# Layer 0's projection stage as one list schedule, from a transposed x that the host lays out, with the norm factors applied to the results

## The chip, the core and the metric

The kernel runs on one core of a Trainium2 chip. Its engines have queues of their own: PE (TensorE) multiplies, DVE (VectorE), ACT (ScalarE) and POOL (GpSimd) do elementwise work, SP (SyncE) here issues the transfers. The metric is device time in microseconds, the median of a few executions, and each profile is of one execution of the same program. In the names of the profile a weight or activation is called by its tile: `hT` are the normalised activations with the model dimension on partitions, `wr` a weight as loaded, `wh` and `wl` its two parts, `psa` and `psb` the accumulators in PSUM (`psa` two buffers of 1024 columns, `psb` four of 512), `qd`, `kd`, `vd`, `kmem`, `vmem` are scratch tensors in DRAM.

## The reference

A decoder trunk of two layers over 1024 tokens of width 1024, in float32. This case touches what stands ahead of layer 0's attention:

```python
def rms_norm(x, g):
    y = xf * lax.rsqrt(jnp.mean(xf * xf, axis=-1, keepdims=True) + EPS)
    return (y * g.astype(jnp.float32)).astype(x.dtype)

# layer 0
h = rms_norm(x, attn_norm[0])
proj = h @ w_in                     # 12 query heads, 6 kinds of keys/values x 2 groups, 36 gates, 4 memory heads
q, k_slc, k_win = rope(...)         # rotary turn of queries and keys
kc = rope(compress_blocks(k_cmp, cmp_pos[0], cmp_w1[0], ...), cmp_end)
vc = compress_blocks(v_cmp, cmp_pos[1], cmp_w1[1], ...)
gates = jax.nn.sigmoid(gate_logit + gate_b)
# each layer also attends into 256 memory tokens
kv = rms_norm(mem, g_mem) @ w_mem_kv
```

`compress_blocks` takes windows of 32 tokens at a stride of 16, adds a position table, and puts them through a small network of two matrices with a GELU between. The factor of the norm is one number for each token, so it may be applied to a row of h or to the row of a product of h. Attention of layer 0 is then the sum of three branches (compressed, selected, window) with 12 heads; then come the output projection, a gated feed-forward block with a convolution, and layer 1 with attention of another kind.

## The kernel before, in words

Each matrix product is made of three: both operands are split into a rounded upper part (ACT writes it) and the rest (DVE or POOL subtracts), and `mm3` (L245) issues upper x upper, upper x lower and lower x upper at L249, L250 and L251 into one accumulator. So every weight costs an ACT copy and a subtraction before PE can use it.

`layer0_proj` (L1135) does layer 0's projections. The tokens come in eight blocks of 128. For each, `norm_x` squares the rows on ACT with a running sum (L210), makes the factor on DVE and POOL (L211, L213) and multiplies row, factor and gain on DVE (L227); `norm_turn` turns the block by eight PE transposes (L242) and splits it into `hT` (L173, L174). After each block come the products for the values and gates (292 columns, `product`), which go to `vd0` through `store_v`. Then six generators take turns in a fixed string of letters (`order`, in `layer0_proj`): the keys and the first four heads' queries (`rope_proj`, L1019, with the rotary turn at L1033 to L1040 and stores at L1044), the two compress networks (`compress`, L1056, products with 256-column operands called `m`) and the keys and values of the memory for both layers (`mem_kv`, L327). All other order, the loads on SP among it, follows from how the generators are written. Near the end the first unit's keys are fetched (`keys0`, L1255).

Attention of layer 0 is planned: `planned` (L697) turns scores (L413, PE), maxima (L443, DVE), exponentials (ACT), transposes of the probabilities (L533) and value products (L557) into tasks with durations, and `Plan.run` (L82) is a list scheduler that puts them out in the order in which they would start. Each engine has one task at a time, and a task may hold buffers (`psa`, `psb`, `wr`, and so on). Between these tasks stand fillers: the projections of the other eight heads and of the memory queries (`rope_tasks`, L901; `plain_tasks`, L859). The units' loads (queries, keys, values: L1291, L1260, L1298) are tasks of SP, of no duration in the plan, and the first of them waits for a task `start` of 15 us.

Pools of tiles in SBUF hand out buffers; a tile that takes a place over waits for the earlier tile there.

Of the kernel before, what the change touches and what calls it, by code (L numbers as in the profile page):

```python
# [43 lines left out]
class Plan:  # L44
# [18 lines left out]
    def can(self, t):  # L63
        free, held = self.free, self.held
        for a in t["acq"]:
# [4 lines left out]
            elif a == "pb":  # L70
                if held.get("pb") or free["psb"] < 2:
# [10 lines left out]
    def run(self):  # L82
        engines = ("SP", "POOL", "DVE", "ACT", "PE")
# [51 lines left out]
class Trunk:  # L135
    def __init__(self, ctx, tc, a, out):
        self.tc, self.nc, self.a, self.out = tc, tc.nc, a, out
        e = ctx.enter_context
        self.cp = e(tc.tile_pool(name="cp", bufs=1))
        self.wp = e(tc.tile_pool(name="wp", bufs=1))  # L140
        self.hp = e(tc.tile_pool(name="hp", bufs=1))
# [37 lines left out]
    def constants(self):  # L179
# [7 lines left out]
        nc.vector.memset(self.m_cau[:, :S - P], 0.0)  # L187
        self.nhalf = c[:, C_NH:C_NH + 1]

    def masks(self, pool, keep):  # L190
        nc, m = self.nc, pool.tile([P, C_TRI - C_CAU], F32, name="masks")
        nc.sync.dma_start(m, self.a["consts"][:, C_CAU:C_TRI])
        nc.vector.tensor_copy(self.m_cau[:, S - P:], m[:, 0:P])

        self.m_win = keep.tile([P, 5 * P], BF16, name="winb")
        nc.vector.memset(self.m_win[:, P:4 * P], 0.0)
        nc.vector.tensor_copy(self.m_win[:, 0:P], m[:, P:2 * P])
        nc.vector.tensor_copy(self.m_win[:, 4 * P:], m[:, 0:P])
        self.m_cmp = keep.tile([P, NT, 64], BF16, name="cmpb")
        nc.vector.tensor_copy(self.m_cmp, m[:, 2 * P:].rearrange("p (t n) -> p t n", t=NT))  # L200
# [14 lines left out]

    def norm_t(self, pool, x, gb, hi, lo, o):

        self.norm_turn(self.norm_x(pool, x, gb), hi, lo, o)
# [34 lines left out]
    def proj_t(self, wcol, h, chunks=2):  # L253

        a = self.psa()
        for c in range(chunks):
            for kt in range(KT):
                self.mm3(a[:, c * CH:(c + 1) * CH], wcol(kt), (h[c][0][:, kt, :], h[c][1][:, kt, :]), kt == 0, kt == KT - 1)
        return a

# [6 lines left out]

    def load_cols(self, w, c0, width=P):

        raw = self.wraw([P, KT, width])  # L270
        self.nc.sync.dma_start(raw, w[:, c0:c0 + width].rearrange("(k p) n -> p k n", p=P))
        hi, lo = self.whl([P, KT, width])
        self.split(raw, hi, lo)
        return lambda kt: (hi[:, kt, :], lo[:, kt, :])
# [1814 lines left out]
```

## Time and profile before

| | us |
|---|---|
| median of 3 executions (2533.4 to 2538.47) | 2537.28 |
| the profiled execution | 2537.82 |
| its span in the profile | 2536.0 |
| PE busy over the span | 2457.5 (97%) |
| DVE, ACT, POOL busy over the span | 1835.6, 1344.0, 796.4 |
| layer 0's projections, to the last product before the first score | 0 to 181.05 |
| attention of layer 0 with fillers | 183 to 473 |
| attention of layer 0 without fillers | 473 to 620 |

In the views quoted below, a group's row reads: line, engine, operation, output<-inputs, shape, count, then busy time and mean ns of one, then the idle time of the engine just before, with what ended it. A row of the timeline reads: start, duration, engine, line, operation, tiles, shape, count, and in brackets the idle time ahead of it and what released it. A matmul's duration includes its way through the array, so neighbours overlap; starts tell the pace. A wait view has the total, the number of times and the longest. SPq is SP's own queue of issues.

### The profile page before, as it was taken

What the parts mean: (1) busy time and instruction counts of PE and PEld (TensorE: products, weight loads), DVE (VectorE), ACT (ScalarE), POOL (GpSimd) and SP (SyncE); (2) the same over time, 40 slices, a digit from 0 to 9 for tenths busy, and PEclk for the clock granted to TensorE, in tenths of its full rate; (3) what the DMA queues carried; (4) which work ended last, traced back from release to release, by engine and by line L of the source; (5) the groups of instructions that cost most, each with busy time, mean ns of one, the idle gap of its engine ahead of it and who ended that gap; (6) DMA issues with size and microseconds to landing.
All of it is one profiled execution on the core that took longest, in us unless ns stands there. A gap on an engine that the chain in (4) does not pass through costs nothing.

```text
span 2536.0 us, 35681 instructions
## 1 busy us (share of the span) xinstructions
PE 2457.5 (97%) x12306; PEld 2051.9 (81%) x12306; DVE 1835.6 (72%) x3078; ACT 1344.0 (53%) x2565; POOL 796.4 (31%) x722
## 2 busy tenths in 40 slices
PE   7899999988999999999999999999999999999998
PEld 6788888776878888888889988887778888888887
DVE  5648787676377787888765467878477777888766
ACT  5338787686254454454454356767235445445444
POOL 2235555476045554540000000000225455451001
PEclk9999999999999999999999999999999999999999
DMA  8473333344323333358335466665632333338523
GB/s 251 140 218 91 93 108 106 88 138 135 136 83 100 100 112 100 100 174 303 96 125 155 151 184 187 186 195 167 217 111 79 100 109 104 100 108 299 175 92 125
DMA packets 303276, 357.68 MB, mean 141 GB/s; under 512 B 38024, under 2 KB 183288, under 8 KB 303096
## 3 DMA queue, kind: packets, MB, share of 16 engines
q1 hardware_dynamic: 303096, 355.41, 44.4%
q8 instruction: 97, 1.59, 0.3%
q14 instruction: 83, 0.68, 0.1%
HBM read 245.55 MB, written 109.78 MB: 140 GB/s over the span
## 4 chain that ended last, share of the span: by engine, by line
PE 79%; DVE 5%; ACT 4%; DMA 3%; issue 2%; POOL 2%; SPq 1%; POOLq 0%; ACTq 0%; DVEq 0%
PE psa L249 12%; PE psa L250 12%; PE psa L251 12%; PE psb L249 10%; PE psb L251 10%; PE psb L250 9%; PE psa L413 5%; PE psb L533 4%; PE psb L557 4%; DVE pt L547 1%; ACT pt L544 1%; PE psb L1367 1%; DVE ps L443 1%; ACT ps L456 1%; DMA wr<-o 1%
## 5 line engine op out<-in xcount | busy, mean ns | idle before, releaser
L173 ACT ACTIVATE wh<-wr 128x512 fp32r<-128x512 f32 (+2 forms) x240 | 181.9, 761 | 309.7 <-PE psb L251 140.7
L1848 DVE SCALAR_TENSOR_TENSOR v<-u,cw,v 128x1023 f32<-128x1023 f32 (+1 forms) x176 | 274.5, 1559 | 69.0 <-ACT v L1846 68.7
L174 DVE TENSOR_TENSOR wl<-wr,wh 128x512 fp32r<-128x512 f32 (+2 forms) x232 | 224.4, 969 | 115.6 <-ACT wh L173 115.0
L547 DVE TENSOR_TENSOR pt<-psb,pt 128x512 fp32r<-128x512 f32 (+2 forms) x380 | 244.5, 660 | 70.4 <-ACT pt L544 68.6
L1846 ACT ACTIVATE v<-u,cw 128x1024 f32<-128x1024 f32 x88 | 109.6, 1246 | 310.4 <-DVE u L1835 283.8
L544 ACT ACTIVATE pt<-psb 128x512 fp32r<-128x512 f32 (+2 forms) x380 | 212.7, 575 | 108.8 <-PE psb L533 72.9
L557 PE MATMUL psb<-pt,vv 128*128 128x512 f32 (+2 forms) x864 | 244.8, 361 | 11.2 <-DVE pt L547 6.5
L213 POOL TENSOR_TENSOR rs<-ss,consts 128x1 f32<-128x1 f32 x40 | 23.7, 593 | 625.9 <-DVE ss L211 416.0
L249 PE MATMUL psa<-hT,wh 128*128 128x512 f32 x560 | 218.3, 390 | 0.0
L251 PE MATMUL psa<-hT,wl 128*128 128x512 f32 x560 | 218.1, 389 | 0.2 <-DVE wl L174 0.2
L250 PE MATMUL psa<-hT,wh 128*128 128x512 f32 x560 | 217.9, 389 | 0.0
L413 PE MATMUL psa<-kk,qq 128*128 128x512 f32 (+4 forms) x792 | 180.4, 347 | 15.2 <-DVE stat L443 6.1
L557 PEld LDWEIGHTS psb<-pt,vv 128*128 128x128 f32 x864 | 144.8, 190 | 33.0 <-DVE pt L547 12.7
L456 ACT ACTIVATE ps<-ps,stat 128x128 f32<-128x128 f32 (+1 forms) x192 | 147.4, 771 | 31.3 <-DVE stat L443 31.0
L443 DVE CUSTOM_DVE_ANT_0 ps<-psa,caub 128x128 f32<-128x128 f32 (+1 forms) x192 | 138.8, 751 | 34.1 <-PE psa L413 31.6
L249 PE MATMUL psb<-hT,wh 128*128 128x512 f32 x384 | 156.7, 408 | 1.7 <-ACT wh L173 1.2
L413 PEld LDWEIGHTS psa<-kk,qq 128*128 128x128 f32 x792 | 123.8, 194 | 38.2 <-DVE stat L443 14.0
L251 PE MATMUL psb<-hT,wl 128*128 128x512 f32 x384 | 151.8, 395 | 0.9 <-POOL wl L174 0.9
L533 PE MATMUL psb<-consts,ps 128*128 128x128 f32 x928 | 147.5, 278 | 4.7 <-DVE pt L547 4.0
L250 PE MATMUL psb<-hT,wh 128*128 128x512 f32 x384 | 151.0, 393 | 0.0
L617 POOL TENSOR_TENSOR wr<-wr 128x512 f32<-128x512 f32 x16 | 21.3, 1329 | 411.2 <-DMA o<-ob 294.2
L249 PE MATMUL psa<-hx,wh 128*128 128x512 f32 x368 | 144.1, 392 | 0.4 <-ACT u L1838 0.4
(322 smaller groups left out, 6784.2 us busy)
## 6 DMA issues: line engine op xcount, KB each, us to landing
wr<-in_w_up_dram SPq DMA_DIRECT2D x88, 512.0 KB
wr<-gd SPq DMA_DIRECT2D x154, 256.0 KB
gd<-v SPq DMA_DIRECT2D x88, 256.0 KB
gd<-gs SPq DMA_DIRECT2D x66, 256.0 KB
o<-ob SPq DMA_DIRECT2D x128, 128.0 KB
wr<-o SPq DMA_DIRECT2D x32, 512.0 KB
hT<-in_w_down_dram SPq DMA_DIRECT2D x64, 256.0 KB
qd<-st SPq DMA_DIRECT2D x56, 256.0 KB
```

The costliest lines, as they stand in the source:

```text
L173: nc.scalar.activation(hi, src, AF.Copy)
L174: (low or nc.vector).tensor_tensor(lo, src, f32(hi), ALU.subtract)
L249: mm(out, lh, rh, start=first, stop=False, skip_group_check=more)
L250: mm(out, lh, rl, start=False, stop=False, skip_group_check=more)
L251: mm(out, ll, rh, start=False, stop=last, skip_group_check=more)
L413: nc.tensor.matmul(out, w, rhs, start=b not in banks[:i], stop=b not in banks[i + 1:])
L456: nc.scalar.activation(p, p, AF.Exp, bias=st[:, 0, ii:ii + 1], scale=-1.0, accum_out=st[:, 1, ii:ii + 1])
L533: nc.tensor.transpose(tp[0:kb, x:x + P], br["pt"][ii][:, o:o + kb], self.ident)
L544: self.nc.scalar.activation(st["hi"], st["src"], AF.Copy)
L547: self.nc.vector.tensor_tensor(st["lo"], st["src"], f32(st["hi"]), ALU.subtract)
L557: self.nc.tensor.matmul(u["o"][:, iis[0] * P:iis[0] * P + w], br["v"](j), t[:, x:x + w], start=st["begin"] and first and i == 0, stop=st[" ...
L1848: nc.vector.scalar_tensor_tensor(v[:, d:], u[:, :S - d], cw[:, tap, i:i + 1], v[:, d:], ALU.mult, ALU.add)
```

## The change

**Layouts.** The host now gives also `x_t` and `mem_t` (x and mem transposed, in tiles), `gcol` (the five gain vectors needed as columns), and the weights of layer 0's input projection, the compress networks' first matrix and position table in tiles as they are used (`layouts`). They are copies and transposes; no number is changed.

**Norms.** A tile of `x_t` has the model dimension on partitions, so h times the gain is one ACT operation for the upper part (scale by a column) and one DVE operation for the rest, and no transposes of x or mem are made. What is multiplied is not normalised. The rows of x and mem are loaded besides, squared on ACT for the sums; POOL raises them to -1/2; and a product of a matrix of ones with a diagonal matrix of the factors spreads them along columns (`spread`, three times: twice four and once two blocks). They are multiplied into the rotary tables on POOL (the queries' tables are kept in DRAM as `rope_r` for the fillers), into the compress networks' input, into the values and gates (per row) and into the memory's keys and values. The memory queries among the fillers get one DVE operation more for it, and their subtraction moves to POOL.

**Schedule.** The whole stage is one `Plan` (`proj_tasks`, `compress_tasks`, `mem_tasks`), transfers included, for which the plan has an engine "DQ" that issues one at a time. The first unit's second keys, values and queries are fetched within it (`ahead`); `start` is gone. The subtractions of the key and query weights, and of every second piece of the compress networks' first matrix and of the memory's weights, are POOL's; masks are filled by POOL. The last layer's memory stores wait until the stage's end (`late_stores`).

**Pools.** All pools in SBUF get `reuse_waits="tile"`, by which a new tile waits for the users of the tiles whose place it takes. Layer 1 takes its gain columns from `gcol` instead of loading and turning them.

```diff
     def run(self):
-        engines = ("SP", "POOL", "DVE", "ACT", "PE")
+        engines = ("SP", "DQ", "POOL", "DVE", "ACT", "PE")
...
-        self.cp = e(tc.tile_pool(name="cp", bufs=1))
+        self.cp = e(tc.tile_pool(name="cp", bufs=1, reuse_waits="tile"))
...
-        start = pl.add("SP", 15.0, lambda: None)
...
-            deps = [(done[n], 6.0) for n in u["needs"]] + [start]
+            deps = [(done[n], 6.0) for n in u["needs"]]
...
-                    s = pl.add("PE", s_us, lambda it=it: self.score(it), [s_prev, (ld, 4.0)], prio, ["psa"])
+                    s = pl.add("PE", s_us, lambda it=it: self.score(it), [s_prev, (ld, 4.0 if k > 1 else 1.0)], prio, ["psa"])
...
+                def hi(e=e, kt=kt):
+                    act(h[c][0][:, kt, :], t["x"][:, e, :], AF.Identity, scale=g[:, kt:kt + 1])
+
+                def lo(e=e, kt=kt):
+                    dve.scalar_tensor_tensor(h[c][1][:, kt, :], t["x"][:, e, :], g[:, kt:kt + 1], f32(h[c][0][:, kt, :]), ALU.mult, ALU.subtract)
...
+            def sq():
+                act(x["x"], x["x"], AF.Square, accum_out=ss[:, j:j + 1])
...
+            def power():
+                gps.tensor_tensor(r, ss, self.nhalf.to_broadcast([P, n]), ALU.pow)
+
+            def diagonal():
+                dg = x["d"] = self.sb(cpool, [P, n, P], F32, "qq1", 2)
+                for j in range(n):
+                    dve.tensor_scalar(dg[:, j, :], self.ident, r[:, j:j + 1], None, ALU.mult)
+
+            def spread():
+                x["p"] = self.psa()[:, 0:n * P]
+                mm(x["p"], ones, x["d"].rearrange("p j q -> p (j q)"), start=True, stop=True)
...
+            out = [add("POOL", 1.3, lambda i=i: gps.tensor_tensor(x[i], x[i], rb[:, cs], ALU.mult), [ld, dep], at - 1) for i in range(2)]
...
+                dve.tensor_tensor(x["u"][:, cs], x["p"][:, cs], rb[:, cs], ALU.mult)
...
+                def lo(b=b, t=t):
+                    (gps if b % 2 else dve).tensor_tensor(t["w"][1], t["r"], f32(t["w"][0]), ALU.subtract)
...
+        for c in range(2):
+            add("DQ", 3.7, lambda c=c: queries(c), qps["d", c] + vd_t + [rt], 111 + c, ["sv", "q1"])
...
+                def scale(c=c):
+                    x["t"] = self.sb(pool, [P, CH], F32, "rt0", 1)
+                    nc.vector.scalar_tensor_tensor(x["t"], x["ps", c, 0], QSC, x["r"], ALU.mult, ALU.mult)
...
-                            got["g"] = self.layer1_gains(vp)
+                            got["g"] = self.gcol[:, 24:40]
```

**Where instructions move.** PE's first rows before (`xn` is a block's normalised rows, `consts` holds the identity):

```order
L242 MATMUL psb_122<-consts,xn_103 128x128 x4
L242 MATMUL psb_129<-consts,xn_103 128x128 x4
L249 MATMUL psb_147<-wh_118,hT_88 128x292
L250 MATMUL psb_147<-wl_119,hT_88 128x292
L251 MATMUL psb_147<-wh_118,hT_89 128x292
```

and PE's first rows now (`mm3` stands at L252 to L254, `m_13` are the key weights' upper part):

```order
L252 MATMUL psb_154<-wh_142,hT_89 128x292
L253 MATMUL psb_154<-wl_143,hT_89 128x292
L254 MATMUL psb_154<-wh_142,hT_90 128x292
L252 MATMUL psb_155<-wh_142,hT_89 128x292
L253 MATMUL psb_155<-wl_143,hT_89 128x292
...
L254 MATMUL psb_157<-wh_142,hT_90 128x292
L252 MATMUL psa_175<-hT_89,m_13_149 128x512
L253 MATMUL psa_175<-hT_90,m_13_149 128x512
```

The first product needs a weight and a scaled tile of `x_t` now, and values of four blocks and keys take turns for each piece of the model dimension.

PE around the first scores before (L413; `wh_1679` are weights of the second four heads' queries):

```order
L249 MATMUL psb_1723<-hT_88,wh_1679 128x512
L250 MATMUL psb_1723<-hT_89,wh_1679 128x512
L251 MATMUL psb_1723<-hT_88,wl_1680 128x512
L413 MATMUL psa_1782<-kk_253_1603,qq_279_1740 128x128
L413 MATMUL psa_1782<-kk_253_1603,qq_280_1741 128x128
```

and now (scores at L337; `m_100` and `m_179` are the scaled memory tokens for layers 0 and 1, and the last row stands directly behind the stage's last product):

```order
L253 MATMUL psb_1183<-m_101_752,wh_1223 128x256
L337 MATMUL psa_1584<-kk_106_820,qq_148_1110 128x128
L337 MATMUL psa_1584<-kk_106_820,qq_149_1111 128x128
L337 MATMUL psa_1584<-kk_106_820,qq_148_1110 128x256
L254 MATMUL psb_1183<-m_100_751,wl_1224 128x256
...
L253 MATMUL psb_1426<-wl_1523,m_179_1301 128x256
L254 MATMUL psb_1426<-wh_1522,m_180_1302 128x256
L337 MATMUL psa_1604<-kk_170_1240,qq_148_1110 128x192
```

The first scores stand among the memory products; the next ones, which need a third buffer of `psa`, stand directly behind the last memory product. DVE there, now (`xl_1553` and `st_1556` take the memory's values and keys for layer 1, L367 are the maxima):

```order
L1495 TENSOR_TENSOR rt_206_1550<-psb_1425,rm 128x256 x2
L1516 SCALAR_TENSOR_TENSOR xl_1553<-psb_1426,rrm,xl_1553 128x4x64
L1502 TENSOR_TENSOR st_1556<-rt_206_1550,st_1556 128x512
L1516 SCALAR_TENSOR_TENSOR xl_1553<-psb_1426,rrm,xl_1553 128x4x64
L367 ISA ps_219_1596,stat_1595<-psa_1584,caub 128x128
```

The maxima of the first scores stand behind the last memory results. SP's queue ahead of the first queries, now (`w_h` is the compress networks' first matrix, `qd_78` the scratch of the queries):

```order
L1328 DMA wr_1013<-in_w_h_dram 128x1024
L1178 DMA qd_78<-st_992 128x512 x2
L1178 DMA qd_78<-st_1011 128x512 x2
L1328 DMA wr_1052<-in_w_h_dram 128x1024
L1825 DMA one<-in_consts_dram 16x8
L1328 DMA wr_1071<-in_w_h_dram 128x1024
L1145 DMA rope_r<-cos_994 128x512
L1145 DMA rope_r<-sin_996 128x512
L1464 DMA wr_1106<-in_w_mem_kv_dram 128x2x512
L1582 DMA qq_148_1110<-qd_78 32x512
```

Stores that wait for results of POOL and DVE stand between loads of weights on the one queue.

More of the change, by code (lines that the diff above doesn't have):

```diff
@@ L70, in can @@
             elif a == "pb":
-                if held.get("pb") or free["psb"] < 2:
+                if free["psb"] < 2 or held.get("pb", 0) > (0 if "psa" in held else 1):
                     return False
@@ L886, in build, with chunk_tasks @@
-                d = pl.add("DVE", 0.7, lo, [a], prio[c * 4 + 3], (), ["pb"])
+                a = pl.add("DVE", 0.7, scale, [pe, (tb, 4.0), d], prio[c * 4 + 3], (), ["pb"])
+                a = pl.add("ACT", 0.55, hi, [a], prio[c * 4 + 3])
+                loaded[0]["turned"] = d = pl.add("POOL", 1.3, lo, [a], prio[c * 4 + 3])
             return pe, d
         return {"name": name, "n": 8, "build": build}
-    def chunk_tasks(self, pl, x, h, c, wcol, pe, prio):
+    def chunk_tasks(self, pl, x, h, c, f, wcol, pe, prio):
@@ L1261, in keys0, with join_keys, values0, queries0 @@
         return kk
+    def join_keys(self, kk, g):
+        self.nc.vector.tensor_copy(kk[:, :, P:], f32(self.kc[:, g, :]).rearrange("p (o n) -> p o n", o=1).to_broadcast([P, NT, 64]))
+        return kk
+    def values0(self, pool, g, b):
+        vv = self.sb(pool, [P, NT, P], F32R, "vv", 2)
+        self.nc.sync.dma_start(f32(vv), self.vd0[:, b * NG + g, :].rearrange("(t p) d -> p t d", p=P))
+        return vv
+    def queries0(self, pool, h, c):
+        q = [self.sb(pool, [P, CH], F32R, f"qq{i}", 2) for i in range(2)]
+        for i in range(2):
+            for half in range(2):
+                for x in range(2):
+                    p0 = (i ^ x) * HD + half * 32
+                    self.nc.sync.dma_start(f32(q[x][p0:p0 + 32, :]), self.qd0[i, half, h * 32:(h + 1) * 32, c * CH:(c + 1) * CH])
+        return q
     def units0(self, ap, cpool):
@@ L1599, in gated @@
             down = Down(self, l, up.gds, fx)
-            with tc.tile_pool(name=f"u{l}", bufs=1) as late, tc.manual_schedule(engines={mybir.EngineType.DVE, mybir.EngineType.Activation}):
+            with tc.tile_pool(name=f"u{l}", bufs=1, reuse_waits="tile") as late, tc.manual_schedule(engines={mybir.EngineType.DVE, mybir.EngineType.Activation}):
                 up.run(late, down)
@@ L2013, in by_tile @@
         self.prep(len(self.steps))
+        rest = None
         for p in range(4):
@@ L2021, in by_tile @@
                 k.nc.vector.tensor_tensor(xs, self.banks[p], xs, ALU.add)
-            then(p)
+            if rest:
+                rest()
+            rest = then(p)
+        rest()
     def add(self, i):
```

896 lines of the change are left out of this document (560 added, 336 removed).

## The prediction

> **What bounds the kernel now.** I read the utilisation windows first, then the first microseconds of the timeline, PE's waits, and last the timeline around the first attention scores. In the windows the columns after the stretch are its length, then busy time with the count in brackets for PE, weight loads, DVE, ACT and POOL, then granted TensorE clock, DMA share and GB/s.
>
> ```profile
> 0.00:20.00 20.00, 9.37 (x50) 7.82 (x51) 10.72 (x21) 10.28 (x18) 1.89 (x7) 1.00 0.84 257
> 20.00:40.00 20.00, 17.63 (x137) 17.21 (x137) 12.74 (x26) 10.38 (x22) 2.44 (x4) 1.00 0.93 273
> 100.00:120.00 20.00, 15.23 (x100) 14.08 (x100) 17.11 (x18) 10.03 (x12) 8.27 (x5) 0.91 0.56 184
> 0.00:181.05 181.05, 158.53 (x929) 138.94 (x929) 100.31 (x166) 75.70 (x124) 51.25 (x45) 0.98 0.66 203
> 200.00:250.00 50.00, 48.99 (x328) 42.76 (x327) 45.23 (x140) 45.21 (x115) 30.22 (x49) 1.00 0.31 81
> 450.00:473.00 23.00, 22.65 (x111) 18.25 (x110) 6.85 (x11) 6.70 (x12) 6.15 (x5) 1.00 0.33 101
> 500.00:550.00 50.00, 44.33 (x288) 37.39 (x287) 37.78 (x95) 40.94 (x107) 35.56 (x46) 0.99 0.43 120
> 1140.00:1170.00 30.00, 30.00 (x133) 24.24 (x132) 26.62 (x39) 13.87 (x23) 0.00 (x0) 1.00 1.04 388
> ```
>
> The projection stage runs to about 181 us. PE is the engine with most to do, and it is not full: holes in the first 40 us and again from 100 on, where the clock drops too. From 200 on PE is full (48.99 of 50) because projections of later heads fill the holes of attention; they last until 473 (22.65 of 23), and without them PE falls to 44.33 of 50. So a microsecond won ahead of 473 moves the last filler forward by a microsecond, and what follows, in the same order, moves with it.
>
> Now PE's pace and how much of those 181 us is work. Starts of neighbours give the pace; the groups give the counts (L249 to L251 have equal counts).
>
> ```profile
> 60.09 0.39 PE L249 MATMUL psa<-hT,wh 128*128 128x512 f32 x1
> 60.32 0.39 PE L250 MATMUL psa<-hT,wh 128*128 128x512 f32 x1
> 146.33 0.28 PE L250 MATMUL psa<-m,wh 128*128 128x256 f32 x1
> 146.45 0.28 PE L251 MATMUL psa<-m,wl 128*128 128x256 f32 x1
> 28.20 1.03 PE L242 MATMUL psb<-consts,xn 128*128 128x128 f32 x8
> L249 PE MATMUL psb<-hT,wh 128*128 128x512 f32 x80 | 32.5, 406 | 1.2 <-ACT wh L173 1.2
> L249 PE MATMUL psa<-hT,wh 128*128 128x512 f32 x32 | 12.5, 390 | 0.0
> L249 PE MATMUL psb<-wh,hT 128*128 128x292 f32 x64 | 20.3, 317 | 0.4 <-ACT wh L173 0.4
> L249 PE MATMUL psb<-wh,m 128*128 128x256 f32 x32 | 9.7, 304 | 0.6 <-DVE m L174 0.6
> L242 PE MATMUL psb<-consts,xn 128*128 128x128 f32 x96 | 13.6, 287 | 12.2 <-DVE xn L227 9.3 <-DVE ss L211 2.4 <-DVE gates L1195 0.5
> ```
>
> A 512-column product starts every 0.2265 us (the mean of several starts; two give 0.23), a 256-column one every 0.117, one of 292 every 0.134 (worked out between the two); eight transposes take 1.03 with the tail of the last, 0.11 each. Work up to 181.05: 336 x 0.2265 = 76.1, 192 x 0.134 = 25.7, 288 x 0.117 = 33.7 (two more forms of 96 read like the one quoted), 96 x 0.11 = 10.5, some 1 of small ones: 147 us. **Lost: 34 us.** The transposes' row shows 12.2 us of waiting for norms; another wait and the start of the timeline:
>
> ```profile
> PE psb L250 <- DVE wl L174: 5.2, 3, 2.8
> 4.17 1.06 ACT L210 ACTIVATE xn<-xl 128x1024 f32<-128x1024 f32 x1 [2.17 <-DMA xl<-in_x_dram]
> 7.62 1.29 DVE L227 SCALAR_TENSOR_TENSOR xn<-xl,rs,gb 128x1024 f32<-128x1024 f32 x1 [2.11 <-DMA gb<-in_attn_norm_dram]
> 8.56 0.69 ACT L173 ACTIVATE wh<-wr 128x584 fp32r<-128x584 f32 x1 [3.25 <-DMA wr<-in_a_w_in_dram]
> 8.96 1.97 PE L242 MATMUL psb<-consts,xn 128*128 128x128 f32 x8 [8.96 <-DVE xn L227]
> 12.62 0.45 PE L249 MATMUL psb<-wh,hT 128*128 128x292 f32 x1
> 13.38 0.30 PE L251 MATMUL psb<-wh,hT 128*128 128x292 f32 x1
> ```
>
> PE starts at 8.96 and is slow until 13.38 (a product takes 0.45, then 0.30), which costs about 2.2 more: a head of 11.2. The other 22.8 is mid-stage: waits on split weights, on norms, and slow stretches behind them.
>
> **The change part by part.** *PE's work.* Its 48 products of the next heads that stood before the first score stand behind it now, which only reorders work ahead of 473. The rest keeps its counts, except that the 96 transposes go (-10.5) and three products with a matrix of ones come (1280 columns; float32 is not seen here in such a product, so its price is bounded by one and by four times the pace, 0.6 to 2.3; I take 2.3). Net **-8.2**.
>
> *The head.* Nothing waits for a norm or a gain row. x comes in 512 KB pieces as before; that data landed at 4.17, and a piece stands one small issue later, so say 4.6. Then two scalings by ACT and the first weights' upper half, 0.69: first product between 6.4 and 7.3, plus 2.2 of slow clock, 9.3 at most instead of 11.2: **-1.9**. Bounds: weights as late as the 8.56 of now give nothing; 6.4 gives -2.6.
>
> *The middle.* Normalised rows, their transposes and the turning chain (L242's 12.2 us of waits, start included) are gone, and the compress chains lie among other products. What can still stop PE: the late weight splits, half on POOL, and loads behind stores on SP's queue. POOL's prices, and the start of attention:
>
> ```profile
> 110.09 1.21 DVE L174 TENSOR_TENSOR wl<-wr,wh 128x1024 fp32r<-128x1024 f32 x1
> 110.25 2.20 POOL L1040 TENSOR_TENSOR rt<-rt,rt 128x512 f32<-128x512 f32 x1 [13.86 <-DVE rt L1039]
> 168.41 2.40 POOL L1241 TENSOR_TENSOR wl<-wr,wh 128x1024 fp32r<-128x1024 f32 x1 [2.23 <-ACT wh L1238]
> 170.98 1.29 POOL L1040 TENSOR_TENSOR rt<-rt,rt 128x512 f32<-128x512 f32 x1 [0.18 <-DMA kmem<-st]
> 180.66 0.39 PE L251 MATMUL psb<-hT,wl 128*128 128x512 f32 x1
> 183.35 2.42 PE L413 MATMUL psa<-kk,qq 128*128 128x128 f32 x8 [2.30 <-DMA qq<-qd]
> 186.75 3.49 PE L413 MATMUL psa<-kk,qq 128*128 128x192 f32 x14 [0.98 <-DVE stat L443]
> 193.24 0.88 PE L413 MATMUL psa<-kk,qq 128*128 128x512 f32 x4 [1.28 <-DMA qq<-qd]
> 185.69 8.50 SPq L1291 DMA_DIRECT2D qq<-qd  x13
> ```
>
> A POOL subtraction takes 1.29 us for 512 columns and 2.40 for 1024, and 2.20 instead of 1.29 where it ran beside DVE: 1.7 times. I count three stalls in the middle: one late split at 2.40, one lengthened to 4.1 (2.40 x 1.7), and one weight as late as the longest of today, 2.8. That is 9.3, between nothing and today's 22.8: **-13.5**. The trade I weighed most is moving subtractions to POOL. The Trainium skill ("SBUF — State Buffer", "Who interferes with whom") says a DVE instruction with two SBUF inputs and a GpSimd instruction that reads SBUF exclude each other for a whole instruction; the 2.20 beside DVE's 1.21 agrees. By that rule DVE loses too when POOL comes first, up to 2.40 a time, which the row does not show; with one such stall of DVE on the path the sum would come out at 2512 instead.
>
> *Transfers.* SP's transfers up to the last weight piece of the memory projection add up to 38.4 MB by the shapes in its order. Work to the end of the projections is 147 - 10.9 - 8.2 + 1.3 for the first scores = 129.2; with head and stalls, 9.3 each, they end near 148. The last piece must land before ACT's copy (about 1.05), POOL's 2.40 and 24 products x 0.117 = 2.8, at 141.5. That asks for 273 GB/s on average, just what 20 to 40 us showed, at a share of 0.93 with narrow slices of weights; wide rows reached 388. I take 330, in between: landed at 117, nothing on the path. Bounds: 203 (this stage's mean) to 388.
>
> *The start of attention.* From 180.66 to 193.24 PE did about 5 us of work in 13: 8 lost, since queries and keys were fetched one issue after another (13 in 8.50 us). Now they are fetched ahead and the first scores lie among the memory products. But DVE takes the memory results before the first maxima, and there are two score buffers:
>
> ```profile
> L174 DVE TENSOR_TENSOR st<-psa,st 128x256 fp32r<-128x256 f32 x4 | 1.7, 420 | 3.0 <-ACT st L173 3.0
> 184.96 0.29 DVE L443 CUSTOM_DVE_ANT_0 ps<-psa,caub 128x128 f32<-128x128 f32 x1 [1.85 <-PE psa L413]
> 185.17 0.42 DVE L443 CUSTOM_DVE_ANT_0 ps<-psa,caub 128x256 f32<-128x256 f32 x1
> 185.52 0.55 DVE L443 CUSTOM_DVE_ANT_0 ps<-psa,caub 128x384 f32<-128x384 f32 x1
> ```
>
> After the last memory product: four 256-column operations at 0.42, a copy and a subtraction of 512 columns (about 1.3), three maxima (0.29 + 0.42 + 0.55), handovers: 4.5 to 5 us until a buffer is free. So 5 instead of 8: **-3** (0 to -8). The Trainium skill ("TensorE: Matmul & The Clock Gate", "Part 1: The HAM clock gate") lets the clock halve after an idle window of some 3.4 us; today's 0.91 over 100 to 120 agrees that holes cost clock. By it this hole would cost up to 1.7 more, an estimate from that page, and the sum would be 2512.
>
> *Waits by tile.* From attention on every engine keeps its order but for the extra scaling of the memory queries on DVE (cover: DVE has 5 of 50 us free beside a full PE; uncovered 2 x 2 x 0.7 = 2.8). About a hundred semaphore waits vanish at pool borders. The largest of PE's there:
>
> ```profile
> PE psb L249 <- ACT hT L173: 3.4, 3, 2.5
> PE psb L1367 <- DVE t L1396: 2.2, 2, 1.1
> ```
>
> Together 5.6, and their data is late in any case; I take **-1** of 0 to -5.6.
>
> **Sum.** 8.2 + 1.9 + 13.5 + 3 + 1 = 27.6 us. The profiled execution took 2537.8, half a microsecond above the median; 2537.8 - 27.6 = **2510 us**.
>
> **Rivals.** *Better:* PE is fed throughout and attention starts without a hole: 9.3 + 5 more, 2496. For it: the stage has only 203 GB/s and DVE 100 of 181 us busy now; against it, every list here so far left holes. *POOL becomes the bound:* from the masks on it has 15 operations of 512 columns, 8 of 504 and 10 of 1024, 15 x 1.29 + 8 x 1.3 + 24 + 2.5 for the masks = 56 us; at 1.7 times 96, from about 62, when the masks are due in the list, to 158, with the last split 13 us after the 145 (148 less its products) at which it is wanted: 2523. *The holes stay:* only their names change, and 13.5 is lost again: 2524. *Nothing:* the holes stay, the head waits for weights, and the scores start no earlier: what is left is 8 of transposes, less the 2.8 of the uncovered memory scaling, about 5: 2533. *Slower:* the transfers are the bound. The rows of x are loaded a second time, tables go to DRAM and back, and all stands in one queue in list order; stores wait for late results with loads behind them. At the 203 GB/s that the stage reaches now, 38.4 MB end at 190, 48.5 after the 141.5, so 2558; it decides from below 228 GB/s (27.6 us late). For it: 0 to 40 us already show shares of 0.84 and 0.93. Against it: 388 with wide rows, and today's queue idles behind DVE.
>
> **How the numbers follow.** The forecast has 0.47, better 0.13, POOL 0.14, holes stay 0.15, nothing 0.05, slower 0.06. A difference under 0.2%, 5 us, can't be told from none here. Faster: 0.47 + 0.13 + 0.14 + 0.15 = 0.89; same 0.05; slower 0.06. The range goes from just under the better case to just over the two weaker gains, 2495 to 2527.
>
> **What would show it.** PE's first product near 7 and no transposes of x; PE over 19 of 20 us in each window from 20 to 140; first score between 110 and 135; last projection product near 148, last filler near 446; POOL's 1024-column operations under 3 us on average; over 280 GB/s between 40 and 120. Wrong would be a PE wait on POOL's split or on DMA above 5 us in sum, or a shift after 473 other than that at 473.

## The result, and the profile after

The changed kernel takes 2520.16 us (median of 4, 2513.84 to 2521.49) against 2537.88 us for the kernel before beside it: a ratio of 0.9926, interval 0.9902 to 0.9949. That is 17.7 us faster, where 27.6 were forecast; 2520 lies in the range. The profiled execution took 2520.44 us, its span 2518.7, so 17.3 us less than the span before. Run again later (the last experiment) it took 2518.18 us, ratio 0.9923 (0.9909 to 0.9936).

The windows of the changed kernel, with the columns as before, show where the stage still has holes; its last product starts at 161.13.

```profile
0.00:20.00 20.00, 11.45 (x53) 10.18 (x54) 5.21 (x8) 10.38 (x16) 3.17 (x8) 1.00 0.82 274
20.00:40.00 20.00, 19.31 (x107) 16.49 (x106) 10.81 (x21) 13.80 (x24) 6.59 (x5) 1.00 0.88 319
60.00:80.00 20.00, 16.68 (x76) 13.90 (x76) 10.76 (x20) 11.46 (x21) 16.00 (x15) 0.91 0.92 316
80.00:100.00 20.00, 20.00 (x89) 16.55 (x89) 17.25 (x20) 5.84 (x8) 8.61 (x8) 1.00 0.65 213
100.00:120.00 20.00, 18.93 (x107) 16.05 (x106) 13.26 (x11) 8.79 (x11) 18.93 (x10) 1.00 0.62 203
120.00:140.00 20.00, 14.54 (x98) 13.73 (x98) 19.89 (x23) 8.67 (x12) 14.52 (x9) 0.83 0.79 222
160.00:180.00 20.00, 15.39 (x79) 13.50 (x79) 12.92 (x42) 15.11 (x35) 11.54 (x15) 0.83 0.62 203
0.00:161.13 161.13, 140.00 (x799) 123.36 (x799) 101.82 (x143) 75.71 (x120) 80.47 (x60) 0.97 0.78 254
```

The kernel before had in two of these stretches:

```profile
60.00:80.00 20.00, 20.00 (x94) 16.65 (x93) 13.81 (x20) 5.31 (x7) 0.55 (x1) 1.00 0.43 102
120.00:140.00 20.00, 17.68 (x112) 15.54 (x111) 10.85 (x22) 7.93 (x14) 4.14 (x4) 0.91 0.73 235
```

PE is fuller than before in 20 to 40 us and in 100 to 120, but there is a hole in 60 to 80, where PE was full before, a larger one in 120 to 140, where DVE is busy for 19.89 of 20 us, and the one at the start of attention. PE's waits up to 200 us, the longest:

```profile
PE psb L252 <- ACT wh L1010: 8.2, 1, 8.2
PE psa L337 <- DVE stat L367: 4.6, 1, 4.6
PE psa L252 <- ACT rb L1069: 4.0, 2, 3.3
PE psb L254 <- DVE cth L1365: 2.6, 1, 2.6
PE psb L254 <- DVE wl L1471: 1.5, 1, 1.5
```

To see where time went I added up, for each stretch, what PE lost: its length less each product that starts in it at its pace (the median distance to the next start: 0.227 us for 512 columns, 0.118 for 256, 0.135 for 292, 0.109 for transposes). The starts are those of the traces.

| lost by PE, us | before | changed | changed, second trace |
|---|---|---|---|
| first 20 us | 14.0 | 11.3 | 11.3 |
| rest of the stage (20 to 181; 20 to 160) | 18.4 | 20.0 | 19.3 |
| start of attention (the next 20 us) | 8.4 | 7.6 | 5.5 |
| attention after it (200 to 620; 180 to 600) | 53.3 | 48.2 | 48.6 |

So 7 of the 17.3 us are lost time, and the other 10 are work that PE no longer has. The 96 transposes at 0.109 are 10.5 of it. The three spread products took about 1.0, 1.0 and 0.6 us, and this sum counts their six records at the pace of the other products, 1.1, which leaves 9.4; the other 1.5 stand among the losses. So the work that went is 10.5 less 2.6, 7.9, close to the 8.2 of the forecast.

A second reading is the lead: the same product in both traces, its start before less its start after. From 720 to 1480 us it is 16.7 to 16.8: what was won by then is carried. Two traces of the same changed kernel differ in it, though, by 2.8 us at 98 us and by 3.3 from the start of attention on, so a lead below that, taken between single traces, tells nothing.

### The profile page after: what moved, and what is told of

Its sections match the earlier page's. It is cut to its first block, busy times and chain, and to the rows that moved or that the text cites. A ratio compares the mean times of both kernels' runs of the same rounds, so it can differ in the third digit from the quotient of the medians.

```text
span 2518.7 us, 35452 instructions
## 1 busy us (share of the span) xinstructions
PE 2444.8 (97%) x12215; PEld 2042.7 (81%) x12215; DVE 1834.8 (73%) x3058; ACT 1348.9 (54%) x2564; POOL 841.2 (33%) x742
## 4 chain that ended last, share of the span: by engine, by line
PE 81%; DVE 7%; ACT 5%; DMA 4%; issue 2%; POOL 1%; SPq 0%; POOLq 0%; ACTq 0%; DVEq 0%
PE psa L252 13%; PE psa L253 12%; PE psa L254 12%; PE psb L252 10%; PE psb L254 10%; PE psb L253 10%; PE psa L337 5%; PE psb L457 4%; PE psb L481 4%; DVE pt L471 1%; ACT pt L468 1%; DMA xl<-in_x_t_dram 1%; DVE ps L367 1%; PE psb L1681 1%; ACT ps L380 1%
## 5 line engine op out<-in xcount | busy, mean ns | idle before, releaser
L173 ACT ACTIVATE wh<-wr 128x512 fp32r<-128x512 f32 (+1 forms) x210 | 155.8, 742 | 273.1 <-PE psb L254 142.4
L174 DVE TENSOR_TENSOR wl<-wr,wh 128x512 fp32r<-128x512 f32 (+1 forms) x210 | 196.9, 938 | 100.0 <-ACT wh L173 99.4
L252 PE MATMUL psa<-hT,wh 128*128 128x512 f32 x592 | 231.7, 392 | 4.4 <-ACT rb L1069 3.3
L253 PE MATMUL psa<-hT,wh 128*128 128x512 f32 x592 | 230.8, 390 | 0.0
L254 PE MATMUL psa<-hT,wl 128*128 128x512 f32 x592 | 230.8, 390 | 0.0
L220 POOL TENSOR_TENSOR rs<-ss,consts 128x1 f32<-128x1 f32 x28 | 17.0, 611 | 564.2 <-DVE ss L218 564.2
L337 PE MATMUL psa<-kk,qq 128*128 128x512 f32 (+4 forms) x792 | 177.8, 342 | 12.2 <-DVE stat L367 9.0
L481 PEld LDWEIGHTS psb<-pt,vv 128*128 128x128 f32 x864 | 145.4, 190 | 29.3 <-DVE pt L471 10.6
L367 DVE CUSTOM_DVE_ANT_0 ps<-psa,caub 128x128 f32<-128x128 f32 (+1 forms) x192 | 138.6, 751 | 25.9 <-PE psa L337 22.9
L2047 POOL TENSOR_TENSOR ws<-wr 128x512 f32<-128x512 f32 x44 | 80.4, 1826 | 216.1 <-DMA wr<-in_w_up_dram 177.0
L337 PEld LDWEIGHTS psa<-kk,qq 128*128 128x128 f32 x792 | 122.5, 192 | 30.1 <-DVE stat L367 14.2
L252 PE MATMUL psb<-wh,hT 128*128 128x512 f32 (+2 forms) x352 | 132.8, 378 | 13.8 <-ACT wh L1010 8.2
L252 PE MATMUL psa<-hx,wh 128*128 128x512 f32 x368 | 144.1, 392 | 0.5 <-ACT u L2144 0.5
L253 PE MATMUL psa<-hx,wh 128*128 128x512 f32 x368 | 143.6, 390 | 0.0
```

The costliest lines, as they stand in the source:

```text
L174: (low or nc.vector).tensor_tensor(lo, src, f32(hi), ALU.subtract)
L252: mm(out, lh, rh, start=first, stop=False, skip_group_check=more)
L253: mm(out, lh, rl, start=False, stop=False, skip_group_check=more)
L254: mm(out, ll, rh, start=False, stop=last, skip_group_check=more)
L337: nc.tensor.matmul(out, w, rhs, start=b not in banks[:i], stop=b not in banks[i + 1:])
L367: self.nc.vector.tensor_tensor_reduce(p, s, br["spans"][ii][2], -1.0, 3e38, ALU.add, ALU.min, br["stat"][:, 0, ii:ii + 1])
```

## The experiments

### Waits by tile alone

```diff
-        self.cp = e(tc.tile_pool(name="cp", bufs=1))
+        self.cp = e(tc.tile_pool(name="cp", bufs=1, reuse_waits="tile"))
   (all 16 pools in SBUF of the kernel before)
```

> The kernel before with the waits by tile alone, nothing else changed. Theory (waits by tile are worth about nothing, since the data they wait for is late anyway): 2537 us, within 2 of the kernel before, and the same idle times of PE behind 620 us. Rival (the waits at pool borders are what the gain behind 473 us in the changed kernel comes from): 5 to 7 us faster, 2531, with PE's lead over the kernel before growing between 473 and 490 us.

2538.73 us against 2537.21, ratio 1.0005 (0.9996 to 1.0014). PE's losses are those of before in every stretch within 1.5 us, and the lead over it is between -0.7 and 1.1 from 175 to 1770 us. In the kernel before these waits are worth nothing.

### The same, taken out of the changed kernel

```diff
-        with tc.tile_pool(name="l0p", bufs=1, reuse_waits="tile") as pool:
+        with tc.tile_pool(name="l0p", bufs=1) as pool:
   (all pools)
```

> The changed kernel without the waits by tile. Theory (they are worth nothing here either): 2520 within 2 us, and the same losses of PE in each stretch. Rival (the new stage's buffers, which change shape more often, need them): the stage ends several us later than 161.

2521.96 us, ratio 0.9937 (0.9922 to 0.9951): by the time within 4 of the changed kernel's two results and not told apart from them. The trace tells more. Up to the end of the stage PE loses what it loses in the changed kernel; then attention's first maxima wait, and the kernel is 3.4 us behind the first trace of the changed kernel and 6.7 behind the second. PE's wait,

```profile
PE psa L337 <- DVE stat L367: 9.4, 1, 9.4
```

and DVE's timeline:

```profile
167.35 0.29 DVE L367 CUSTOM_DVE_ANT_0 ps<-psa,caub 128x128 f32<-128x128 f32 x1 [3.83 <-DMA vmem<-xl]
```

DVE has the first scores before it and stands 3.83 us for the store of the memory's values for layer 1, which attention does not need: the new pool's tiles lie where the stage's tiles lay. With waits by tile this wait is not there, and PE waits 4.1 to 4.6 us at that place instead of 9.4. So, by the traces, the option takes some 5 us of waiting off one border in the new stage and gives nothing in the old kernel; the rival was right that the new stage needs it, though not about the place, since the stage does not end later.

### The attention plan alone

```diff
   (the kernel before, with the changed kernel's chunk_tasks, rope_tasks and plain_tasks, whose tables are not scaled)
-        start = pl.add("SP", 15.0, lambda: None)
-            deps = [(done[n], 6.0) for n in u["needs"]] + [start]
+            deps = [(done[n], 6.0) for n in u["needs"]]
-                    s = pl.add("PE", s_us, lambda it=it: self.score(it), [s_prev, (ld, 4.0)], prio, ["psa"])
+                    s = pl.add("PE", s_us, lambda it=it: self.score(it), [s_prev, (ld, 4.0 if k > 1 else 1.0)], prio, ["psa"])
```

> The kernel before with the change's attention plan alone: the fillers' tasks (weights of 1024 columns as one copy and one subtraction, host layouts for them, memory queries with one more DVE operation), no start task, the plan's new condition on two accumulators; the projection stage and the pools stay. PE's order in attention is the changed kernel's from its 182nd row on. Theory (7 of the 17 us come from attention's order around the last fillers, not from the projection stage): 2530 us, the last filler near 473 as before or a little earlier, and PE 6 to 8 us ahead of the kernel before behind it. Rival (all of the gain is the projection stage's): 2537, no lead behind the last filler.

2545.46 us, ratio 1.0026 (1.0015 to 1.0037): slower, and both numbers were wrong. The first scores in PE's waits up to 200 us,

```profile
PE psa L413 <- DMA qq<-qd: 15.0, 2, 14.2
```

and on its timeline:

```profile
186.37 2.70 PE L413 MATMUL psa<-kk,qq 128*128 128x128 f32 x8 [14.24 <-DMA qq<-qd]
```

The products of the next heads, which stood ahead of the first scores and covered the fetching of queries and keys, now stand behind them, and the fetching is bare. In 160 to 200 us PE loses 20.0 us instead of 8.5. From 200 to 500, though, it loses 17.6 instead of 25.1. Without the changed kernel's early fetches the new plan costs time.

### The new fillers with the old start

```diff
   (as above, but)
+        start = pl.add("SP", 15.0, lambda: None)
+            deps = [(done[n], 6.0) for n in u["needs"]] + [start]
+                    s = pl.add("PE", s_us, lambda it=it: self.score(it), [s_prev, (ld, 4.0)], prio, ["psa"])
```

> The kernel before with the change's filler tasks alone, and the plan's start task, its wait of 4 us and its condition on accumulators left as before; so the first scores stand behind the next heads' first products again (PE's 855th row), and PE's order is the changed kernel's from the 794th row of attention on. Theory (the new fillers lose PE 6 to 7 us less within attention, and the earlier kernel with the new plan was slow only because the first queries' transfers stood bare for 14 us): 2531 us, a lead of 5 to 7 over the kernel before from 500 us on. Rival (the new fillers themselves cost time): 2540 or more.

2535.45 us, ratio 0.9988 (0.9978 to 0.9998), 12 runs. The lead over the kernel before is -1.0 at 197 us and 3.4 to 4.0 between 620 and 1750. So the new form of the fillers (weights of 1024 columns in one copy and one subtraction, accumulators free earlier, and the list order that follows) gains some 2 us by the medians (0.5 to 5.6 by the interval) and 4.4 to 5.0 by the one trace. That is less than the 5 to 7 expected, and it has nothing to do with the projection stage.

### Without the second load of x by rows

```diff
-                nc.sync.dma_start(x["x"], src)
-                act(x["x"], x["x"], AF.Square, accum_out=ss[:, j:j + 1])
+                act(x["x"].rearrange("p (k n) -> p k n", k=8), self.ident.rearrange("p (o n) -> p o n", o=1).to_broadcast([P, 8, P]), AF.Square, accum_out=ss[:, j:j + 1])
```

> The changed kernel without the second load of x and mem by rows (5.2 of 38.4 MB); ACT squares the identity instead, as many elements, so the norm factors are those of other numbers. Theory (transfers set only the one late load of query weights near 63 us): the wait of 3.3 us for the spread factors there and the slow clock behind it shrink, the hole between 120 and 140 us stays; the stage ends near 157 instead of 161, the kernel at 2516. Rival (transfers are the bound of the stage): 5.2 MB at some 240 GB/s are 22 us, the stage ends near 140 and the kernel at 2500.

2520.19 us, ratio 0.993 (0.9917 to 0.9944): no difference that the times show. In its trace the stage keeps its holes; two of its windows:

```profile
20.00:40.00 20.00, 19.31 (x106) 16.36 (x105) 9.90 (x21) 11.96 (x22) 5.31 (x4) 1.00 0.48 167
120.00:140.00 20.00, 15.39 (x107) 14.87 (x106) 19.91 (x26) 9.48 (x14) 14.35 (x7) 0.83 0.81 230
```

The DMA share in 20 to 40 us falls from 0.88 to 0.48, and PE is as busy as with the loads, 19.31. Its lead from 177 us on is 2.2 over the first trace of the changed kernel and -1.1 over the second: nothing, where my theory wanted 4 and the rival 20. PE's wait for the spread factors near 62 us is 2.3 here, as in the second trace (2.1). Transfers are not the bound of the stage; the forecast's slower rival is out.

### POOL's late operations made into fills

```diff
-                (gps if b % 2 else dve).tensor_tensor(t["w"][1], t["r"], f32(t["w"][0]), ALU.subtract)
+                (gps.memset(f32(t["w"][1]), 0.0) if b % 2 else dve.tensor_tensor(t["w"][1], t["r"], f32(t["w"][0]), ALU.subtract))
   (and the position adds of POOL likewise)
```

> The changed kernel with POOL's late subtractions (every second piece of the compress networks' and the memory's weights) and its half of the position adds made into fills with zero, which read nothing from SBUF; those parts of the operands are zero then. DVE's instructions are the same, in the same order. Theory (POOL and DVE hold each other up while both read two operands from SBUF, and that makes the hole between 117 and 137 us): DVE's subtraction of 1024 columns there goes from 2.1 to 2.5 us back to 1.2, its position adds from 1.5 to 0.7, PE's waits of 5.5 us there and most of the slow clock go, the stage ends near 152, the kernel at 2512. Rival (DVE just has too many operations there): their durations and the hole stay, the kernel within 2 us of 2520.

2512.49 us, ratio 0.9899 (0.9884 to 0.9914), 6 to 8 us below the changed kernel's two results, as the theory said; three of the four executions lie below all nine of the changed kernel. DVE's groups in the changed kernel:

```profile
L1306 DVE TENSOR_TENSOR kk<-vv,cpos 64x504 f32<-64x504 f32 x8 | 11.8, 1480 | 0.2
L1335 DVE TENSOR_TENSOR wl<-wr,wh 128x1024 fp32r<-128x1024 f32 x4 | 9.1, 2265 | 0.9 <-ACT wh L1332 0.9
```

and with the fills (the lines moved by three):

```profile
L1309 DVE TENSOR_TENSOR kk<-vv,cpos 64x504 f32<-64x504 f32 x8 | 8.2, 1023 | 0.2
L1338 DVE TENSOR_TENSOR wl<-wr,wh 128x1024 fp32r<-128x1024 f32 x4 | 4.9, 1234 | 4.2 <-ACT wh L1335 4.1
```

and the window that held the hole:

```profile
120.00:140.00 20.00, 19.22 (x160) 18.93 (x160) 19.32 (x40) 13.10 (x25) 8.55 (x7) 1.00 0.93 292
```

The same DVE instructions, 1.23 us instead of 2.27 and 1.02 instead of 1.48 where POOL only writes. (The adds did not fall to the 0.7 that I took from the kernel before: there they read PSUM.) PE loses 1.0 us in 120 to 140 instead of 8.6 and 8.1, and from 100 to 138 us it gains 7.6 on both traces of the changed kernel. Its lead over them is 10.0 and 7.2 at 138 us and 7.5 and 4.2 behind the start of attention (the hole there is larger for it, 6.3 us of waiting). The fills also shorten POOL's own operations, 2.4 to 0.96 for a subtraction, but most of the gain is DVE's: from the subtraction of L1315 at 117.91 to the first copy into `cdup` at 134.68 DVE has no gap that counts, and that stretch takes 16.8 us in both traces of the changed kernel and 10.0 with the fills, for the same operations. Over the whole stage, up to the first maxima, DVE's 147 operations add up to 114.0 and 113.6 us in the changed kernel and to 97.3 with the fills. In the changed kernel the two engines stand on each other's instructions; DVE, then POOL, over that stretch:

```profile
120.64 3.02 DVE L1306 TENSOR_TENSOR kk<-vv,cpos 64x504 f32<-64x504 f32 x2
123.69 2.14 DVE L1335 TENSOR_TENSOR wl<-wr,wh 128x1024 fp32r<-128x1024 f32 x1
126.09 0.68 DVE L1155 TENSOR_TENSOR rt<-psa,cos 128x512 f32<-128x512 f32 x1
126.69 2.45 DVE L1471 TENSOR_TENSOR wl<-wr,wh 128x1024 fp32r<-128x1024 f32 x1
129.06 1.21 DVE L1315 TENSOR_TENSOR m<-kk,m 128x1024 fp32r<-128x1024 f32 x1
132.33 2.42 DVE L1387 TENSOR_TENSOR crt<-cres,ct 128x32 f32<-128x32 f32 x1
...
120.73 4.02 POOL L1306 TENSOR_TENSOR kk<-vv,cpos 64x504 f32<-64x504 f32 x2
124.83 3.22 POOL L1335 TENSOR_TENSOR wl<-wr,wh 128x1024 fp32r<-128x1024 f32 x1
132.32 2.39 POOL L1471 TENSOR_TENSOR wl<-wr,wh 128x1024 fp32r<-128x1024 f32 x1
```

An operation of 32 columns (0.18 us a moment earlier) takes 2.42 beside a POOL subtraction that starts 0.01 us earlier and takes 2.39. A DVE subtraction takes 2.45 us when POOL is in the way and 1.21 when it is not. The one that reads PSUM runs beside POOL in 0.68.

### POOL's late operations on DVE

```diff
-                (gps if b % 2 else dve).tensor_tensor(t["w"][1], t["r"], f32(t["w"][0]), ALU.subtract)
+                dve.tensor_tensor(t["w"][1], t["r"], f32(t["w"][0]), ALU.subtract)
   (and the position adds likewise)
```

> The changed kernel with POOL's late work (8 subtractions of 1024 columns, 8 position adds) on DVE. By their price alone these are 8 x 1.21 + 8 x 0.68 = 15 us more for DVE between 100 and 150. Theory (POOL's reads hold DVE up by about as much as POOL takes over): DVE's operations there return to 1.2 and 0.7 us, so DVE ends these operations no more than 3 us later, and the kernel stays within 3 of 2520. Rival (the split over two engines is worth its price): DVE becomes the bound by some 10 us, 2530.

2520.57 us, ratio 0.9929 (0.991 to 0.9947): no difference to the changed kernel, with 16 operations more on DVE. Its groups on DVE,

```profile
L1306 DVE TENSOR_TENSOR kk<-vv,cpos 64x504 f32<-64x504 f32 x16 | 16.3, 1021 | 0.3
L1335 DVE TENSOR_TENSOR wl<-wr,wh 128x1024 fp32r<-128x1024 f32 x8 | 11.2, 1409 | 0.8 <-ACT wh L1332 0.7
```

and one of PE's waits:

```profile
PE psb L254 <- DVE cth L1365: 2.9, 1, 2.9
```

Twice as many subtractions of the compress weights take DVE 11.2 us instead of 9.1, twice the adds 16.3 instead of 11.8, and the memory weights' eight subtractions take 10.6 where four took 6.1. DVE's other operations become shorter, so all of its operations of the stage add up to 115.9 us for 163 of them, against 114.0 and 113.6 for 147. So of the 18 us of work that the change gave to POOL here (16 operations at 1.02 and 1.23), DVE paid nearly all in waiting. PE's hole is as large (7.8 us lost in 120 to 140): DVE is the bound there with either split.

### The wait at 62 us

```diff
-            p = add("ACT", 1.05, hi, [ld], 66 + b, ["w"])
+            p = add("ACT", 1.05, hi, [ld, row_t[1]], 66 + b, ["w"])
```

> The changed kernel with the upper half of the first four heads' query weights put behind the copy of the spread factors in ACT's order, one dependency more in the plan. Theory (the stall at 62 us is ACT's queue: the copy of the factors stands behind a weight copy whose load is late): PE's wait of 3.3 us falls under 1, the slow clock behind it goes, the loss between 60 and 80 us falls from 5.3 to about 1.5, and the lead of 3.5 to 4 us arrives at 160 us. Rivals: the late load stops PE later by as much (no lead at 100), or DVE's hole between 117 and 137 eats it (a lead at 100, none at 160).

In the changed kernel ACT and PE stand like this:

```profile
63.74 1.06 ACT L1211 ACTIVATE wh<-wr 128x1024 fp32r<-128x1024 f32 x1 [2.79 <-DMA wr<-in_w_r_dram]
64.70 0.58 ACT L1069 ACTIVATE rb<-psa 128x512 f32<-128x512 f32 x1
65.33 0.79 PE L252 MATMUL psa<-hT,wh 128*128 128x512 f32 x1 [3.32 <-ACT rb L1069]
```

The copy of the spread factors out of PSUM had its data, but stood in ACT's queue behind a copy whose weights were still on their way. With the dependency that wait falls to 0.7, yet the kernel takes 2528.2 us in the one execution, 8 above the changed kernel, and is, by the first trace, 2.9 us behind at 98 us and 6.8 from 200 us on. PE loses 7.4 us in 60 to 80 instead of the expected 1.5. One dependency more moved the whole list; PE's waits between 60 and 120 us are now others:

```profile
PE psb L253 <- POOL wl L1335: 4.7, 2, 2.7
PE psa L252 <- DVE qq L1155: 2.8, 1, 2.8
PE psa L252 <- DVE vv L1291: 2.2, 1, 2.2
```

So the queue is shown for this wait, and what the wait costs is not, since no two lists differ in it alone.

### The table load ahead of x

```diff
+        warm = pool.tile([P, 1], F32, name="warm")
+        hot = add("POOL", 0.1, lambda: gps.memset(warm, 1.0), [], -30)
+        add("ACT", 0.2, lambda: act(warm, warm, AF.Square), [hot], -30)
```

> The changed kernel with one more ACT operation on a filled column ahead of everything else, so that ACT's table load no longer stands behind the first piece of x (4.96 to 6.24 us now). Theory (the table load is 1.3 us of the head): first product near 7.0 instead of 8.22, a lead of 1.2 us over the changed kernel that stays to the end of the stage. Rival (the first weights' landing sets the first product): ACT's copy of the weights starts at 7.5 as now, no lead.

> The changed kernel with the early table load, timed against the kernel before. Its single profile kept a lead of 2.3 us over the changed kernel from 177 us on. Theory (a lead won ahead of attention arrives whole): 2518 us, ratio 0.992 to 0.9925. Rival (the first look was one lucky run): 2520 as the changed kernel.

The start of ACT's timeline in the kernel before, in the changed kernel, and in this one:

```profile
0.72 1.28 ACT L210 ACT_TABLE_LOAD   x1 [0.72 <-PEq L2077]
```

```profile
4.96 1.28 ACT L994 ACT_TABLE_LOAD   x1 [4.96 <-DMA xl<-in_x_t_dram]
6.26 1.33 ACT L994 ACTIVATE hT<-xl,gcol 128x512 fp32r<-128x512 f32 x2
```

```profile
0.72 1.28 ACT L979 ACT_TABLE_LOAD   x1 [0.72 <-PEq L2414]
4.57 1.33 ACT L997 ACTIVATE hT<-xl,gcol 128x512 fp32r<-128x512 f32 x2 [2.36 <-DMA xl<-in_x_t_dram]
```

The table load stands behind the wait for the first x in the changed kernel; before, it was done at 2.00, although ACT's first operation waited for x until 4.17 there too. What puts the load behind the wait in one kernel and not in the other is not shown. The first product starts at 6.54 and 7.1 us in the two traces instead of 8.22 and 8.1, so the head's part is as the theory has it. Whether it arrives, the traces cannot tell: at 175 us these two are 1.0 and 1.3 us behind the second trace of the changed kernel and 2.3 and 2.0 ahead of the first, which I had taken for the gain. The time is 2514.53 us (5 executions), ratio 0.9912 (0.9899 to 0.9926), the lowest of the complete kernels, but its interval and the changed kernel's 0.9909 to 0.9936 overlap: a gain over the changed kernel is neither shown nor excluded.

### True durations in the plan

```diff
-                p = add("POOL" if b % 2 else "DVE", 1.95 if b % 2 else 1.22, lo, [p], ...)
+                p = add("POOL" if b % 2 else "DVE", 2.4 if b % 2 else 1.9, lo, [p], ...)
   (with the position adds at 1.95 and 1.48, two more of DVE, and the table load ahead)
```

> The same, and in the projection stage's plan the durations of DVE's and POOL's late operations as the trace of the changed kernel shows them (subtractions of 1024 columns 1.9 and 2.4 instead of 1.22 and 1.95, position adds 1.48 and 1.95 instead of 0.66 and 1.3, two more of DVE). Only the order changes. Theory (the list overbooks DVE between 117 and 137 us because it takes durations that hold only without POOL beside): PE's loss between 100 and 140 us falls from about 10 to 5 or less, 2513 us. Rival (the work and the buffers, not the order, make the hole): the loss stays at 10 or moves to another stretch, 2516 to 2520.

2515.74 us, ratio 0.9918 (0.9904 to 0.9931), no better than the early table load alone. PE loses 9.5 us in 100 to 140 (10.3 and 10.4 in the changed kernel, 8.9 in the timed one with the early table load); one wait is replaced by another:

```profile
PE psb L1397 <- DVE cdup L1393: 3.7, 1, 3.7
```

and the adds, which the list now puts together in another way, take 1.95 on DVE in the mean, where the plan had been given 1.48. So the durations of one list did not hold in the next.

### The changed kernel again

> The changed kernel once more, for a second trace and a tighter time. Several kernels whose list is the same up to 100 us lost 3.8 to 4.5 us of PE in 60 to 80 us where its first trace lost 5.3. If that stretch varies from one execution to the next, the second trace differs from the first by up to 2 us there and leads of 2 us taken against the first trace show nothing; if it does not, the second trace has 5.3 again within 0.5, and those leads stand. Time: 2518 to 2521 either way.

2518.18 us, ratio 0.9923 (0.9909 to 0.9936); the profiled execution took 2514.9. PE loses 3.5 us in 60 to 80 where the first trace had 5.3, and idles 4.1 instead of 4.6 at the start of attention. PE's wait near 62 us is 2.1 here and 3.3 in the first trace, and the granted clock of 60 to 80 is 1.00 here and 0.91 there. The stretch varies, so the leads of about 2 us above show nothing. What repeats is the hole: 8.1 and 8.6 lost in 120 to 140, with the same two waits.

```profile
PE psb L254 <- DVE cth L1365: 2.6, 1, 2.6
PE psb L254 <- DVE wl L1471: 1.3, 1, 1.3
```

## Why the prediction was right or wrong

**The number** held its range, at the side of the rivals: 2520 lies between the forecast's 2510 and the 2523 and 2524 of "POOL becomes the bound" and "the holes stay". By mechanism "the holes stay" is what happened in the stage, and attention, which I had excluded, gave part of it back; that the two together fall inside the range is in part luck. POOL did not become the bound: it is busy for 18.93 of 20 us in 100 to 120, but up to 200 us PE waits for it nowhere in the first trace and 0.3 us in the second. Of the signs that I named, the last product of the stage comes at 161.13 instead of near 148, and PE is not over 19 of 20 us in 60 to 80 and 120 to 140.

**PE's work**, -8.2: right, 7.9 by the transposes that went and the spread products that came (2.6 us, where I took 2.3).

**The head**, -1.9: 2.7 in the first 20 us. The first product stands at 8.22, not 6.4 to 7.3, because the table load had moved behind the wait for x, a cost that I did not look for; the products right behind it run on without the gaps of before, which gave more than I counted.

**The middle**, -13.5: this step failed. I let 9.3 of 22.8 us stay; by the same sum of losses it was 18.4 before and 20.0 and 19.3 after. The stalls that I named (norms, turning, compress) did go: no wait on normalised rows, 1.7 us lost in 100 to 120 instead of 7.1. In their place stand the wait at 62 us for the copy of the spread factors, 5.3 and 3.5 lost in 60 to 80, and the DVE hole, 8.6 and 8.1 in 120 to 140 (5.5 us of waits on DVE in the first trace, the rest in the main the clock of 0.83). I had priced POOL's subtractions by what POOL takes (2.40, or 1.7 times that), and the row with 2.20 beside DVE's 1.21 as a loss of POOL alone. The fills show that the larger part is DVE's loss, 6.8 us in the one stretch. The Trainium skill ("SBUF — State Buffer", "Who interferes with whom") had said so: a DVE instruction with two SBUF inputs and a GpSimd one that reads SBUF exclude each other, and a DVE instruction with at most one SBUF input, outside its two-port modes, does not contend. This case agrees on both, 2.45 us beside POOL and 1.21 alone, and 0.68 for the operand in PSUM. I had let that rule weigh one stall of 2.40 us; it was most of the hole's 8.

**Transfers**: right that they are hidden; 5.2 MB less changed nothing in the times. The late load of query weights that ACT waits for near 62 us is of the kind that I had counted in the middle with 2.8; PE waits 3.3 and 2.1 us there. It waits as long for it without the rows (2.77 us of ACT's), so what makes that load late stays open.

**The start of attention**, 8 to 5: it idles for 4.61 us as worked out, but then the clock is low (0.83 over 160 to 180), and 7.6 are lost. In the second trace, whose last product stands at 158.97, 6.4 are lost in the 20 us from there, 4.1 of them idle.

```profile
161.13 0.28 PE L254 MATMUL psb<-wh,m 128*128 128x256 f32 x1
166.01 3.52 PE L337 MATMUL psa<-kk,qq 128*128 128x192 f32 x14 [4.61 <-DVE stat L367]
169.32 0.68 PE L252 MATMUL psb<-hT,wh 128*128 128x512 f32 x1
```

A product of 512 columns takes 0.68 behind the hole and 0.39 when warm. The Trainium skill ("TensorE: Matmul & The Clock Gate", "Part 1: The HAM clock gate") let me expect up to 1.7 more; it was 3.0 and 2.3 with the scores' own gaps. The traces agree with it in kind, and my estimate from it was low: the granted clock is 0.50 from 164.1 to 170.8 us, and from 164.4 to 167.7 in the second trace. A wait of 2.56 us, shorter than the 3.4 that I had reckoned with, was enough for it at 126 us (0.50 from 126.6 to 133.2).

**Attention**: "every engine keeps its order" was wrong. The filler tasks have another form, so the list comes out differently, and PE loses about 5 us less between the start of attention and its end; the new fillers with the old start show 2 of it by their time, and more by their one trace. I read the order where it agrees, behind attention, and took it for all.

**Waits by tile**, -1: 0 in the kernel before, some 5 in the new stage, not at the places that I named but at the one border where a late store would have stopped DVE.

**That a microsecond won before 473 us arrives at the end** held where attention's list is the same: leads of 7.5 and 24.5 us at 200 us (the fills over the changed kernel, the changed kernel over the attention plan alone) are still 7.4 and 24.4 at 500. What is won earlier in the stage need not arrive behind it: of the 10.0 us that the fills lead by at 138 us, 7.5 are left behind the start of attention. Whether the head's microsecond arrives is not shown. My marker was bad, however: the last filler is 10.3 us earlier in the changed kernel (462.7 for 473.1), not 17, because scores stand between the last fillers now. The forecast's "last filler near 446" would have read the result wrongly.

## What to carry to other kernels

Before work is moved from DVE to POOL to unload it, look at what each reads: where both read two operands from SBUF they take turns, and here the move gained nothing that the times show; DVE's operations that read one operand from PSUM ran beside POOL at their usual 0.68 us. Compare two kernels by the lead of the same product, not by a marker such as the last filler. Price a change of plan together with the transfers that must come earlier for it. Take two traces of the same kernel before a lead of a few microseconds is read as an effect.

## What the runs showed of the hardware

- A DVE operation of 128x32, 0.18 us alone, takes 2.42 us beside a POOL subtraction of 2.39; a DVE subtraction of 128x1024 takes 1.21 to 1.23 alone and 2.14 to 2.70 where POOL's came first, and POOL's own 2.39 becomes 3.22. A fill by POOL (it reads nothing) does not lengthen DVE's operations: 1.23. A DVE cast of 128x512, with one operand, took 1.87 us beside a POOL subtraction and 0.42 in the kernel with those subtractions on DVE.
- A float32 product with the matrix of ones appears as two records for each 512 columns, about 1.0 us together.
- ACT's table load can stand behind a transfer: it starts at 4.96 us behind the wait for x in the changed kernel, and at 0.72 in the kernel before and where an operation without such a wait stands first.
- In the changed kernel's first trace the granted clock of PE is 0.50 behind waits of 3.32, 2.56 and 4.61 us (from 65.1 to 68.4, 126.6 to 133.2 and 164.1 to 170.8 us). The wait near 62 us is 2.05 us with the fills and 2.06 in the changed kernel's second trace: the clock then is 0.50 from 64.2 to 67.4 us in the one, and stays at 1.00 in the other.
